# Blocks 0 and 1 of a streaming-encoder layer attended and merged as one pair, with group 1's norm and first projections woven elsewhere

## The chip, the core and the metric

The kernel runs on one core of one Trainium2 chip. The metric is the time on the device in microseconds (us), the median of several runs of the same program. TensorE is called PE below, VectorE DVE, ScalarE ACT, GpSimd POOL and SyncE SP. PE has two clock levels, 1.2 and 2.4 GHz; the profile shows the granted clock as a share of the higher one.

## What is computed

One encoder layer on 1024 frames of width 1024 (batch 1), in float32:

```python
xn = rmsnorm(x, norm1_w);  proj = xn @ w_in            # 1024 x 6656
qd, kd, vd, qc, kc, vc, gd, gc = split(proj)
o_d = diff_attention(qd, kd, vd)   # 8 heads, two softmax maps, chunk-causal, distance bias
o_c = chunk_attention(qc, kc, vc)  # 8 heads, own chunk of 64 frames and the 8 before
h = x + (sigmoid(gd + b) * (o_d @ w_branch_diff) + sigmoid(gc + b) * (o_c @ w_branch_chunk)) @ w_out
# product-key experts: 8 heads, top 16 of 128 x 128 keys, 16384 experts u, v of width 1024
q = rmsnorm(h) @ peer_wq;  s1, s2 = q_halves @ keys
e, g = top16(top16(s1) + top16(s2)), softmax of their scores
h = h + sum_k gelu(u[e_k] . rmsnorm(h)) * g_k * v[e_k]
y = rmsnorm(h, final_norm_w)
```

## The kernel before

The 1024 frames are 8 blocks of 128. `GROUPS` (line 33) makes blocks 0 and 1 group 0 and blocks 2 to 7 group 1.

*Projections.* `norm1` loads a group's rows of x through the three buffers `wr` that weights use too, norms, transposes and splits them in a high and a low part (`xh`, `xl`). `Dense` then has 52 steps per group, one for each 128 columns of `w_in`: load 512 KB of weights, split them in `wh` (ACT, line 128) and `wl` (DVE, line 129), 24 matmuls per piece of up to 512 frames (`mm3`, line 136), write the result to DRAM. `upto(n)` does the steps up to the n-th, `run()` one at each turn.

*Attention.* `attention` (line 304) works through 8 heads of the first kind and 4 head pairs of the second, for a list of blocks: scores on PE (line 347), softmax on DVE and ACT, transposes (line 203), values (line 372). `need(h)` has the projections of head h done first.

*Merge.* `merge` (line 478) takes the outputs `on` and `ocx` of its blocks through `w_bd`, `w_bc`, `w_out` (8 weight loads each; matmuls in plain float32, line 490, as many columns as it has frames; the trace holds two records for each of these matmuls), adds x, norms, and runs the 8 heads of `wq` with `top16` on DVE. `sel` runs `choose` for each block: the final top 16 and, for the blocks of `SBLK` (0, 1, 6, 7), the expert numbers `ei` (line 639).

*Experts.* Blocks 2 to 5 go through all experts densely (`gates`, `dense_experts`). Blocks 0, 1, 6, 7 gather theirs: `experts` issues 128 gathers from u and 128 from v per block on POOL (line 801), 512 KB each into five buffers, and DVE makes one product of each (lines 807 and 818). It is written at the end of the program, but a scheduler places each engine's instructions by when their inputs are ready, so the gathers of blocks 0 and 1 run from the moment that `ei` is there: 448 of them before block 6's turn, since half of block 1's v comes after block 6's u.

*The order of the work.* `weave(main, n, side, m)` runs `m` steps of a side generator over `n` steps of the main one. The order before is in the lines at the end of `layer_kernel`:

```python
weave(att_one(wk, 0, yza), 13, (dn[0].run(), 46))   # line 883
weave(merge(mp, 0, [0], yza, *ons[0]), 25, (att_one(wk, 1, yz1), 13))
run(sel([0], yza))
weave(merge(mp, 0, [1], yz1, *ons[1]), 25, (norm1(1, x1), 6))
run(sel([1], yz1))
dn[1].upto(6)
weave(att_pair(wk, 1, yza), 25, (dn[1].run(), 46))
```

Behind that come the attention of blocks 4 to 7 woven with the merge and selections of blocks 2 and 3, then the merges of blocks 4, 5 and of blocks 6, 7 (`mop`) woven with the gates, then the dense experts. Engines work through their queues in order, so an instruction that waits holds up all behind it on its engine.

Of the kernel before, what the change touches and what calls it, by code (L numbers as in the profile page):

```python
# [12 lines left out]
AF = mybir.ActivationFunctionType  # L13
OP = mybir.AluOpType

P = 128
# [35 lines left out]
def weave(main, n, *sides):  # L52

    at = [0] * len(sides)
    i = 0
    for _ in main:
        i += 1
        for k, (g, m) in enumerate(sides):
            while at[k] < m * min(i, n) // n:
                next(g, None)  # L60
                at[k] += 1
    for g, _ in sides:
        for _ in g:
            pass
# [8 lines left out]
def layer_kernel(ctx, tc, x, w1, w_in, b_gate, lq1, lk1, lq2, lk2, subln, rel,  # L73
                 w_bd, w_bc, w_out, w2, wq, keyst, u, v, ut, wf, identd, dmd, iotad, out):
    nc = tc.nc
# [4 lines left out]
    yza = ctx.enter_context(tc.tile_pool(name="yza", bufs=1))  # L80
# [11 lines left out]
    sub = con.tile([P, 1], F32, name="sub")  # L92
# [119 lines left out]
    def norm1(gi, xp):  # L212

        T = len(GROUPS[gi]) * P
        xh = xp.tile([P, KC, T], F32R, name="xh", tag="xh")
        xl = xp.tile([P, KC, T], F32R, name="xl", tag="xl")
        for i, b in enumerate(GROUPS[gi]):
            xt = wp.tile([P, KC, P], F32, name="xt", tag="wr", bufs=WBUFS).rearrange("p a b -> p (a b)")
            nc.sync.dma_start(xt, x[b * P:(b + 1) * P, :])
            xs = wp.tile([P, KC, P], F32, name="xs", tag="wl").rearrange("p a b -> p (a b)")  # L220
            ss = sm.tile([P, 1], F32, name="ss", tag="ss")
            nc.scalar.activation(xs, xt, AF.Square, accum_out=ss)
            r = rsqrt(sm, ss, 1, 1.0 / D)
            nc.scalar.activation(xs, xt, AF.Copy, scale=r)
            for g in range(2):
                o = transposes([xs[:, (4 * g + j) * P:(4 * g + j + 1) * P] for j in range(4)])
                for j in range(4):
                    c = 4 * g + j
                    oj = o[:, j * P:(j + 1) * P]
                    hi, lo = xh[:, c, i * P:(i + 1) * P], xl[:, c, i * P:(i + 1) * P]  # L230
                    nc.scalar.activation(hi, oj, AF.Copy, scale=w1c[:, c:c + 1])
                    nc.vector.scalar_tensor_tensor(lo, oj, w1c[:, c:c + 1], hi.bitcast(F32), op0=OP.mult, op1=OP.subtract)  # L232
            yield
        dn[gi].x = (xh, xl)

    class Dense:
# [24 lines left out]
        def upto(self, n):  # L261
            while self.done < min(n, len(self.steps)):
                self.steps[self.done]()
                self.done += 1

        def run(self):
            while self.done < len(self.steps):
                self.upto(self.done + 1)
                yield
# [554 lines left out]
    dn = [None, None]  # L824
    ons = {}

    def outputs(yz, T):
        return (yz.tile([P, KC, T], F32, name="on", tag="y"), yz.tile([P, 4, T], F32, name="ocx", tag="z"))

    def att_one(wk, b, yz):  # L830
        on, ocx = ons[b] = outputs(yz, P)
        yield from attention(wk, 2 * P, 0, [b], 1, lambda h: dn[0].upto(3 * h + 3),
                             lambda h, i, t: nc.scalar.activation(on[:, h, :], t, AF.Copy, scale=sub),
                             lambda h, i, t: nc.scalar.copy(ocx[:, h, :], t))

    def att_pair(wk, k, yz):
        on, ocx = ons[k] = outputs(yz, 2 * P)
        yield from attention(wk, (2 * k + 2) * P, 1, [2 * k, 2 * k + 1], 2, lambda h: dn[1].upto(3 * h + 3),
                             lambda h, i, t: nc.scalar.activation(on[:, h, :], t, AF.Copy, scale=sub),
                             lambda h, i, t: nc.scalar.copy(ocx[:, h, :], t))  # L840

# [18 lines left out]
    def sel(blocks, yz):  # L860
        for b in sorted(blocks, key=lambda b: b not in DBLK):
            yield from choose(yz, b)
# [5 lines left out]
    def pool(name):  # L868
        return tc.tile_pool(name=name, bufs=1)

    def wpool(name):
        return tc.tile_pool(name=name, bufs=2)

    with pool("x1") as x1, pool("stp") as stp:
        dn[1] = Dense(1, stp)
        dn[0] = Dense(0, stp)
        with pool("yz1") as yz1, wpool("at0") as wk:
            with pool("x0") as x0:
                run(norm1(0, x0))
                dn[0].upto(3)  # L880
                setup()
                dn[0].upto(6)
                weave(att_one(wk, 0, yza), 13, (dn[0].run(), 46))
            with pool("mp0") as mp:
                weave(merge(mp, 0, [0], yza, *ons[0]), 25, (att_one(wk, 1, yz1), 13))
                run(sel([0], yza))
                weave(merge(mp, 0, [1], yz1, *ons[1]), 25, (norm1(1, x1), 6))
            run(sel([1], yz1))
        with wpool("at1") as wk:
            dn[1].upto(6)  # L890
            weave(att_pair(wk, 1, yza), 25, (dn[1].run(), 46))
    with pool("yzb") as yzb, pool("mp") as mp:
        d1 = [k for k in range(ND) if DBLK[k] < 4]
        d2 = [k for k in range(ND) if DBLK[k] >= 4]
# [66 lines left out]
```

## Time and profile before

| | |
|---|---|
| median of 3 runs | 3340.01 us (3337.91 to 3341.29) |
| the profiled execution | 3344.66 us, span 3342.9 us |
| PE busy (matmuls; weight loads) | 3083.5 us, 92%; 2551.2 us, 76% |
| DVE busy | 2689.5 us, 80% |
| ACT busy | 1430.6 us, 43% |
| POOL busy | 1289.7 us, 39% |
| moved by DMA | 987.11 MB, 295 GB/s in the mean |
| chain that ended last | PE 71%, DVE 11%, DMA 5%, ACT 5%, issue 5% |

The span runs from the first to the last instruction on the core; the profiled execution's own time is 1.8 us longer. Busy shares are means over stages with different limits, so they say little about one stage; a table by stretches of the span does. A busy PE is not PE at its peak, because matmuls are pipelined. A wait is put down to the instruction whose signal came last.

### The profile page before, as it was taken

How to read it: one execution, taken by the hardware profiler on the slowest of the kernel's cores; microseconds unless marked ns; L12 is line 12 of the kernel's file. 1: busy time of each engine (PE TensorE's matmuls, PEld its weight loads, DVE VectorE, ACT ScalarE, POOL GpSimd, SP SyncE). 2: the span in 40 equal slices, each digit the busy share in tenths (PEclk: the TensorE clock that was granted, in tenths of full speed). 3: DMA queues.
4: the chain of work that ended last, by engine and by line, in shares of the span. 5: the costliest groups of instructions: out<-in, count | busy, mean ns of one | idle time of the engine just before them, and what ended most of it. 6: DMA issues, size and time to landing. Idle time of an engine off the chain costs nothing.

```text
span 3342.9 us, 48089 instructions
## 1 busy us (share of the span) xinstructions
PE 3083.5 (92%) x16032; PEld 2551.2 (76%) x16032; DVE 2689.5 (80%) x5720; ACT 1430.6 (43%) x2901; POOL 1289.7 (39%) x1028
## 2 busy tenths in 40 slices
PE   7987689999979988898887789999999999999998
PEld 7986578888866665577776678888888888888886
DVE  4436797787769999975785999888899888889998
ACT  6634433333323444558849833233323233223233
POOL 0000445555544442320000035555465555555553
PEclk9998899999989986899898899999999999999999
DMA  7775989999998995765444579999999999999997
GB/s 239 222 240 185 364 315 351 340 336 343 321 353 317 335 319 179 255 207 199 177 163 159 197 272 361 347 341 340 332 343 352 341 349 339 340 352 346 344 348 251
DMA packets 406120, 987.11 MB, mean 295 GB/s; under 512 B 43184, under 2 KB 188400, under 8 KB 403696
## 3 DMA queue, kind: packets, MB, share of 16 engines
q0 software_dynamic: 147456, 536.94, 45.2%
q1 hardware_dynamic: 258416, 447.11, 38.5%
q8 instruction: 126, 2.06, 0.2%
q14 instruction: 122, 1.00, 0.1%
HBM read 905.72 MB, written 78.15 MB: 294 GB/s over the span
## 4 chain that ended last, share of the span: by engine, by line
PE 71%; DVE 11%; DMA 5%; ACT 5%; issue 5%; POOL 2%; SPq 0%; DVEq 0%; POOLq 0%; ACTq 0%
PE ph L136 18%; PE mm L136 17%; PE acc L710 13%; PE mm L490 8%; PE acc L717 4%; PE sc L347 4%; PE pv L372 3%; PE tr L203 2%; POOL ge L801 2%; PE gg L669 2%; DVE junk L807 1%; ACT gst L671 1%; DMA ge<-in_u_dram,ei 1%; DVE p L353 1%; DVE iu L560 1%
## 5 line engine op out<-in xcount | busy, mean ns | idle before, releaser
L801 POOL DMA_INDIRECT ge<-in_u_dram,ei x512 | 634.0, 1238 | 1419.0 <-DVE ei L639 830.4
L801 POOL DMA_INDIRECT ge<-in_v_dram,ei x512 | 655.5, 1280 | 603.6 <-DVE acc L818 397.3
L818 DVE SCALAR_TENSOR_TENSOR acc<-ge,a,acc 128x1024 f32<-128x1024 f32 x512 | 655.6, 1280 | 24.3 <-DMA ge<-in_v_dram,ei 17.5
L807 DVE SCALAR_TENSOR_TENSOR junk<-ge,xs 128x1024 bf16<-128x1024 f32 x512 | 624.4, 1219 | 47.3 <-DMA ge<-in_u_dram,ei 41.3
L129 DVE TENSOR_TENSOR wl<-wr,wh 128x1024 fp32r<-128x1024 f32 x232 | 283.3, 1221 | 178.7 <-ACT wh L128 111.5
L128 ACT CAST wh<-wr 128x1024 fp32r<-128x1024 f32 x232 | 243.9, 1051 | 412.4 <-PE ph L136 304.4
L136 PE MATMUL ph<-x2h,wh 128*128 128x512 f32 x1024 | 400.4, 391 | 10.0 <-DVE x2l L129 7.0
L136 PE MATMUL ph<-x2l,wh 128*128 128x512 f32 x1024 | 399.8, 390 | 0.0
L136 PE MATMUL mm<-xh,wh 128*128 128x256 f32 (+1 forms) x1248 | 374.0, 325 | 0.7 <-ACT st L286 0.5
L136 PE MATMUL mm<-xl,wh 128*128 128x256 f32 (+1 forms) x1248 | 368.6, 321 | 1.2 <-DVE xl L232 1.2
L136 PEld LDWEIGHTS mm<-xh,wh 128*128 128x128 f32 x1248 | 236.3, 190 | 25.1 <-ACT st L286 3.1
L136 PE MATMUL ph<-x2h,wl 128*128 128x512 f32 x1024 | 253.9, 389 | 0.0
L136 PEld LDWEIGHTS mm<-xl,wh 128*128 128x128 f32 x1248 | 235.9, 189 | 21.2 <-DVE xl L232 1.9
L128 ACT CAST vh<-vr 128x1024 fp32r<-128x1024 f32 x128 | 128.5, 1052 | 249.5 <-PE acc L717 226.5
L136 PE MATMUL mm<-xh,wl 128*128 128x256 f32 (+1 forms) x1248 | 235.1, 324 | 0.0
L136 PEld LDWEIGHTS ph<-x2h,wh 128*128 128x128 f32 x1024 | 193.3, 189 | 51.0 <-DVE x2l L129 7.4
L136 PEld LDWEIGHTS ph<-x2l,wh 128*128 128x128 f32 x1024 | 193.3, 189 | 40.1
L136 PEld LDWEIGHTS ph<-x2h,wl 128*128 128x128 f32 x1024 | 192.2, 188 | 39.7
L347 PE MATMUL sc<-kt,qt 64*128 64x256 f32 (+3 forms) x608 | 200.5, 533 | 16.2 <-DMA kt<-kd 6.9
L128 ACT CAST ah<-ge 128x512 fp32r<-128x512 f32 x128 | 79.6, 622 | 310.0 <-DVE ge L747 309.9
L136 PEld LDWEIGHTS mm<-xh,wl 128*128 128x128 f32 x1248 | 185.2, 189 | 16.8
L710 PE MATMUL acc<-vh,ah 128*128 128x512 f32 x768 | 197.6, 389 | 0.0
(203 smaller groups left out, 5725.9 us busy)
## 6 DMA issues: line engine op xcount, KB each, us to landing
vr<-in_v_dram SPq DMA_DIRECT2D x128, 512.0 KB, 6.8
wr<-in_ut_dram SPq DMA_DIRECT2D x128, 512.0 KB, 6.1
wr<-in_w_in_dram SPq DMA_DIRECT2D x104, 512.0 KB, 5.0
gdr<-gst SPq DMA_DIRECT2D x16, 2048.0 KB, 7.8
gj<-gdr SPq DMA_DIRECT2D x512, 64.0 KB, 6.3
wr<-in_w_bd_dram SPq DMA_DIRECT2D x40, 512.0 KB, 3.8
wr<-in_w_out_dram SPq DMA_DIRECT2D x40, 512.0 KB, 7.0
wr<-in_wq_dram SPq DMA_DIRECT2D x40, 512.0 KB, 5.3
```

Of the source, the lines that this page charges most:

```text
L128: nc.scalar.copy(hi, raw)
L129: nc.vector.tensor_sub(lo, raw, hi.bitcast(F32))
L136: nc.tensor.matmul(o, w[a][:, k, :], xx[b][:, k, :], start=(i == 0), stop=(i == last))
L203: nc.tensor.transpose(o[:, i * P:(i + 1) * P], s, ident)
L347: nc.tensor.matmul(o[:, :k1 - k0], q, k[:, k0:k1], start=True, stop=True)
L372: nc.tensor.matmul(o[:, :P], aT[:, j - c, :], vt[:, v0 + j, :], start=(j == 0), stop=(j == n - 1))
L490: nc.tensor.matmul(o, w[:, k, :], xx[:, k, :], start=(k == 0), stop=(k == K - 1))
L710: nc.tensor.matmul(acc[i][hf], a[x][:, i * P:(i + 1) * P], b[y][:, hf * 512:hf * 512 + 512], **kw)
L717: nc.tensor.matmul(o, aa[:, 3 * P:4 * P], bb[:, cs], start=(n == 0), stop=(n == len(todo) - 1))
L801: nc.gpsimd.indirect_dma_start(out=t, out_offset=None, in_=src, in_offset=bass.IndirectOffsetOnAxis(ap=ei[:, k:k + 1], axis=0))
L807: nc.vector.scalar_tensor_tensor(junk, t, 1.0, xs, op0=OP.mult, op1=OP.mult, accum_out=hid[:, k:k + 1])
L818: nc.vector.scalar_tensor_tensor(acc, t, a[:, k:k + 1], acc, op0=OP.mult, op1=OP.add)
```

## The change

Blocks 0 and 1 are attended as a pair (`att_pair` with k = 0, group 0) in the first stage and merged as a pair with 256 columns. Group 1's norm is woven with that one merge. The selections of both blocks run behind it, woven with eight of group 1's projection steps (the new `some`), and the other 44 steps are woven with the attention of blocks 2 and 3. The second set of output buffers (`yz1`) goes.

```diff
--- before.py
+++ after.py
@@ -262,6 +262,11 @@
             while self.done < min(n, len(self.steps)):
                 self.steps[self.done]()
                 self.done += 1
+
+        def some(self, n):
+            for _ in range(n):
+                self.upto(self.done + 1)
+                yield
 
         def run(self):
             while self.done < len(self.steps):
@@ -827,15 +832,10 @@
     def outputs(yz, T):
         return (yz.tile([P, KC, T], F32, name="on", tag="y"), yz.tile([P, 4, T], F32, name="ocx", tag="z"))
 
-    def att_one(wk, b, yz):
-        on, ocx = ons[b] = outputs(yz, P)
-        yield from attention(wk, 2 * P, 0, [b], 1, lambda h: dn[0].upto(3 * h + 3),
-                             lambda h, i, t: nc.scalar.activation(on[:, h, :], t, AF.Copy, scale=sub),
-                             lambda h, i, t: nc.scalar.copy(ocx[:, h, :], t))
-
     def att_pair(wk, k, yz):
         on, ocx = ons[k] = outputs(yz, 2 * P)
-        yield from attention(wk, (2 * k + 2) * P, 1, [2 * k, 2 * k + 1], 2, lambda h: dn[1].upto(3 * h + 3),
+        gi = min(k, 1)
+        yield from attention(wk, (2 * k + 2) * P, gi, [2 * k, 2 * k + 1], 2, lambda h: dn[gi].upto(3 * h + 3),
                              lambda h, i, t: nc.scalar.activation(on[:, h, :], t, AF.Copy, scale=sub),
                              lambda h, i, t: nc.scalar.copy(ocx[:, h, :], t))
 
@@ -874,21 +874,17 @@
     with pool("x1") as x1, pool("stp") as stp:
         dn[1] = Dense(1, stp)
         dn[0] = Dense(0, stp)
-        with pool("yz1") as yz1, wpool("at0") as wk:
-            with pool("x0") as x0:
-                run(norm1(0, x0))
-                dn[0].upto(3)
-                setup()
-                dn[0].upto(6)
-                weave(att_one(wk, 0, yza), 13, (dn[0].run(), 46))
-            with pool("mp0") as mp:
-                weave(merge(mp, 0, [0], yza, *ons[0]), 25, (att_one(wk, 1, yz1), 13))
-                run(sel([0], yza))
-                weave(merge(mp, 0, [1], yz1, *ons[1]), 25, (norm1(1, x1), 6))
-            run(sel([1], yz1))
+        with wpool("at0") as wk, pool("x0") as x0:
+            run(norm1(0, x0))
+            dn[0].upto(3)
+            setup()
+            dn[0].upto(6)
+            weave(att_pair(wk, 0, yza), 25, (dn[0].run(), 46))
+        with pool("mp0") as mp:
+            weave(merge(mp, 0, [0, 1], yza, *ons[0]), 26, (norm1(1, x1), 6))
+        weave(sel([0, 1], yza), 18, (dn[1].some(8), 8))
         with wpool("at1") as wk:
-            dn[1].upto(6)
-            weave(att_pair(wk, 1, yza), 25, (dn[1].run(), 46))
+            weave(att_pair(wk, 1, yza), 25, (dn[1].run(), 44))
     with pool("yzb") as yzb, pool("mp") as mp:
         d1 = [k for k in range(ND) if DBLK[k] < 4]
         d2 = [k for k in range(ND) if DBLK[k] >= 4]
```

In the program as built, PE has 224 fewer merge matmuls: 448 of 128 columns become 224 of 256. SP issues 89 DMAs fewer, among them 8 loads each of `w_bd`, `w_bc`, `w_out` and `wq`. POOL's queue is the same. DVE has 4597 instructions instead of 4632. Three places show what moves.

On PE, where the first stage ends and the merge of block 0 begins (`on` and `ocx` are the two attention outputs, `wr` a weight tile, `p` and `pv` block 1's attention), before:

```order
L490 MATMUL mm<-on,wr 128x128 x8
L490 MATMUL mm<-ocx,wr 128x128 x4
L203 MATMUL tr<-ident,oh 128x128
L347 MATMUL sc<-kt,qt 128x256 x2
L203 MATMUL tr<-ident,p_2878 128x128 x2
L347 MATMUL sc<-kt,qt 128x256
L490 MATMUL mm<-on,wr 128x128 x8
L490 MATMUL mm<-ocx,wr 128x128 x4
L372 MATMUL pv<-vt,aT 128x128 x2
L347 MATMUL sc<-kt,qt 128x256 x3
```

and now, where the merge of both blocks begins:

```order
L377 MATMUL pv<-vt,aT 128x128 x2
L203 MATMUL tr<-ident,och 128x128
L495 MATMUL mm<-on,wr 128x256 x8
L495 MATMUL mm<-ocx,wr 128x256 x4
L495 MATMUL mm<-on,wr 128x256 x8
L495 MATMUL mm<-ocx,wr 128x256 x4
L495 MATMUL mm<-on,wr 128x256 x8
L495 MATMUL mm<-ocx,wr 128x256 x4
```

The attention of block 1 no longer stands between the merge's matmuls, and these have 256 columns.

On DVE, where `ei` of block 0 is made, before (`xl` is group 1's norm, `g` and `mT` the merge of block 1):

```order
L619 TENSOR_TENSOR sel<-ohib 128x64
L508 SCALAR_TENSOR_TENSOR g_4168<-g_4168,mm 128x128
L232 SCALAR_TENSOR_TENSOR xl<-tr,w1c,xh 128x128
L637 SCALAR_TENSOR_TENSOR row<-sel 128x128
L232 SCALAR_TENSOR_TENSOR xl<-tr,w1c,xh 128x128
L639 CAST ei<-row 128x128
L510 SCALAR_TENSOR_TENSOR g_4168<-g_4168,mm 128x128
L232 SCALAR_TENSOR_TENSOR xl<-tr,w1c,xh 128x128
L511 TENSOR_TENSOR mT<-g_4168 128x128
```

and now (`wl` is a weight split of group 1's projections, `p` its attention, `junk` a product of a gathered tile):

```order
L644 CAST ei<-row 128x128
L129 TENSOR_TENSOR wl<-wr,wh 128x1024
L604 SCALAR_TENSOR_TENSOR row<-s_4674,s_4673 128x128
L358 ISA p_5128,mn<-sc,dm 128x384
L358 ISA mn 128x1
L605 TENSOR_SCALAR s_4674<-row 128x128
L617 TENSOR_TENSOR ohib<-pos,iotaj 128x1024
L606 SCALAR_TENSOR_TENSOR s_4673<-row,s_4674 128x128
L395 RECIPROCAL rz_5142<-z 128x1
L619 TENSOR_TENSOR ohib<-ohib 128x1024
L608 TENSOR_TENSOR pos<-pf,s_4673 128x128
L812 SCALAR_TENSOR_TENSOR junk,hid<-ge,xs_26496 128x1024
```

It now stands behind the seventh of group 1's 52 weight splits, and before stood ahead of the first; `ei` of block 1 stands behind the eleventh, and before behind the ninth.

On DVE, in the merge of blocks 4 and 5 (`xr`) with the gates (`o`), before:

```order
L663 TENSOR_SCALAR o_13911<-iota,it_12459 128x128 x2
L521 TENSOR_TENSOR xr<-xr,tr 128x2x128
L653 TENSOR_TENSOR o_13926<-iota,it_12459 128x512
L663 TENSOR_SCALAR o_13928<-iota,it_12459 128x128 x2
L653 TENSOR_TENSOR o_13961<-iota,it_12459 128x512
L663 TENSOR_SCALAR o_13963<-iota,it_12459 128x128 x2
L521 TENSOR_TENSOR xr<-xr,tr 128x2x128
```

and the same place now (`acc` is a product of a gathered tile):

```order
L526 TENSOR_TENSOR xr<-xr,tr 128x2x128
L823 SCALAR_TENSOR_TENSOR acc<-ge,a,acc 128x1024
L658 TENSOR_TENSOR o_13328<-iota,it_11861 128x512
L668 TENSOR_SCALAR o_13330<-iota,it_11861 128x128 x2
L658 TENSOR_TENSOR o_13363<-iota,it_11861 128x512
L668 TENSOR_SCALAR o_13365<-iota,it_11861 128x128 x2
L823 SCALAR_TENSOR_TENSOR acc<-ge,a,acc 128x1024 x2
L526 TENSOR_TENSOR xr<-xr,tr 128x2x128
L658 TENSOR_TENSOR o_13380<-iota,it_11861 128x512
L668 TENSOR_SCALAR o_13382<-iota,it_11861 128x128 x2
L823 SCALAR_TENSOR_TENSOR acc<-ge,a,acc 128x1024 x2
```

Products of block 1's gathers now stand among the gates. Counted along DVE's queue, the 448 products ahead of block 6's lie so: before, 270 up to the merge of blocks 2 and 3, 140 from there to the merge of blocks 4 and 5, 38 behind that and all of them ahead of its first gate; now 210, 142 and 93, of which 42 lie ahead of the last attention block and 51 among the gates, and 3 later.

## Rows read from the trace of the kernel before

**Rows 1.** The page, part 1: busy us (share of span) x instructions.

```profile
PE 3083.5 (92%) x16032; PEld 2551.2 (76%) x16032; DVE 2689.5 (80%) x5720; ACT 1430.6 (43%) x2901; POOL 1289.7 (39%) x1028
```

**Rows 2.** Busy time by stretch: PE, PEld, DVE, ACT, POOL, granted clock, DMA share, GB/s.

```profile
24.00:198.00 174.00, 170.88 (x1389) 164.36 (x1389) 79.70 (x163) 104.13 (x242) 0.00 (x0) 1.00 0.71 222
198.00:438.00 240.00, 173.91 (x1183) 153.94 (x1183) 151.00 (x616) 96.46 (x288) 44.82 (x42) 0.87 0.78 274
438.00:966.00 528.00, 526.43 (x3053) 443.36 (x3052) 411.14 (x706) 201.19 (x417) 284.21 (x228) 1.00 0.95 335
966.00:1380.00 414.00, 350.96 (x1596) 242.56 (x1595) 370.72 (x1142) 172.68 (x414) 160.51 (x146) 0.85 0.83 285
1380.00:1474.00 94.00, 89.94 (x528) 63.83 (x527) 85.64 (x206) 53.70 (x140) 33.11 (x33) 1.00 0.82 272
1474.00:1610.00 136.00, 116.28 (x664) 102.96 (x663) 63.20 (x158) 104.92 (x247) 0.00 (x0) 0.91 0.52 179
1610.00:1930.00 320.00, 254.02 (x1467) 220.34 (x1466) 260.12 (x1139) 239.85 (x544) 0.00 (x0) 0.89 0.51 180
1930.00:3343.00 1413.00, 1395.83 (x6144) 1155.30 (x6144) 1257.00 (x1563) 441.55 (x576) 766.87 (x576) 0.99 0.94 335
```

**Rows 3.** Waits of PE, 198 to 438: us in total, times, longest.

```profile
PE tr L203 <- ACT xs L224: 19.4, 4, 7.1
PE tr L203 <- DVE xs L530: 9.8, 2, 5.7
PE sc L547 <- ACT st L542: 7.9, 4, 4.5
PE mm L490 <- DMA wr<-in_w_bd_dram: 6.8, 3, 2.9
PE mm L490 <- DMA wr<-in_w_out_dram: 5.8, 5, 1.5
```

**Rows 4.** Waits of POOL, 0 to 1000.

```profile
POOL ge L801 <- DVE ei L639: 339.8, 1, 339.8
```

**Rows 5.** PE groups, 198 to 438: count, busy us, mean ns, idle before.

```profile
L347 PE MATMUL sc<-kt,qt 64*128 64x256 f32 x40 | 11.2, 419 | 0.8 <-DMA qt<-qd 0.8
L372 PE MATMUL pv<-vt,aT 128*128 128x128 f32 x61 | 10.3, 289 | 2.1 <-ACT aT L370 1.3 <-ACT och L451 0.8
L203 PE MATMUL tr<-ident,p 128*128 128x128 f32 x14 | 3.0, 298 | 0.0
L203 PE MATMUL tr<-ident,pc 128*128 128x128 f32 x16 | 2.9, 276 | 0.1
L203 PE MATMUL tr<-ident,oh 128*128 128x128 f32 x8 | 2.5, 312 | 0.9 <-ACT oh L401 0.9
```

**Rows 6.** Busy time of line 490's matmuls alone, in two stretches.

```profile
198.00:438.00 240.00, 128.20 (x896) 118.95 (x896) 0.87 0.78 274
1380.00:1658.00 278.00, 105.27 (x446) 82.52 (x447) 0.96 0.63 217
```

**Rows 7.** Busy time of DVE, ACT, POOL on gathered tiles alone, by stretch.

```profile
438.00:966.00 528.00, 288.10 (x330) 0.00 (x0) 284.21 (x228) 1.00 0.95 335
966.00:1380.00 414.00, 177.97 (x264) 0.00 (x0) 160.51 (x146) 0.85 0.83 285
1380.00:1474.00 94.00, 48.52 (x38) 0.00 (x0) 33.11 (x33) 1.00 0.82 272
```

**Rows 8.** DVE groups, 1380 to 1610: the gather product.

```profile
L818 DVE SCALAR_TENSOR_TENSOR acc<-ge,a,acc 128x1024 f32<-128x1024 f32 x38 | 48.5, 1277 | 0.0
```

**Rows 9.** The page, part 3: the gathers' DMA queue.

```profile
q0 software_dynamic: 147456, 536.94, 45.2%
```

**Rows 10.** Busy time from 350 to 400.

```profile
350.00:400.00 50.00, 31.64 (x204) 29.19 (x205) 34.90 (x80) 25.33 (x70) 22.30 (x20) 0.83 1.01 392
```

**Rows 11.** DVE groups: a merge product of 128 columns (299 to 438), of 256 (1380 to 1610).

```profile
L508 DVE SCALAR_TENSOR_TENSOR g<-g,mm 128x128 f32<-128x128 f32 x8 | 2.3, 285 | 7.0 <-PE mm L490 6.6 <-DMA g<-gd 0.4
L508 DVE SCALAR_TENSOR_TENSOR g<-g,mm 128x256 f32<-128x256 f32 x8 | 3.3, 418 | 9.4 <-PE mm L490 9.4
```

## The prediction

> **What bounds the kernel now.** I read the page first: TensorE (PE) is busy for 92% of the span [rows 1]. That is a mean over stages, so the next view is the table of stretches [rows 2]. The reader is to see three kinds of stage there. From 24 to 198 us (group 0's projections with block 0's attention) and from 438 to 966 us (group 1's projections) PE is busy for all but 3 and 2 us: PE sets the pace, while VectorE (DVE) is busy for 80 of 174 us in the first. From 198 to 438 us, where blocks 0 and 1 are merged one after the other, PE is busy for only 174 of 240 us at a granted clock of 0.87, between its two levels of 1.2 and 2.4 GHz: it idles for 66 us. From 966 to 1380 us DVE is busy for 371 of 414 us and PE for 351. From 1474 to 1610 us there is room: DVE is busy for 63 of 136 us, the DMA engines for 0.52 of the time.
>
> What PE waits for between 198 and 438 us is in the waits [rows 3]: the normed rows of norm1 (19.4 us) and of the merge's second norm (9.8), a staged query (7.9), and weights of the 128-column matmuls (6.8 and 5.8). The expert gathers start when `ei` of block 0 is ready: POOL idled 339.8 us for it [rows 4]. From there DVE's queue holds one product per gathered tile, in a fixed order.
>
> **The change part by part.** Durations are of the profiled execution, 3344.66 us long with a span of 3342.9; the median of the runs shown is 3340.01, 4.65 lower. The sum is made against 3344.66 and the forecast is then put 4.65 lower.
>
> 1. *Attention of block 1 moves from the merge of block 0 into the first stage.* On PE it is the score, value and transpose groups, 11.2 + 10.3 + 3.0 + 2.9 + 2.5 = 30 us [rows 5]. The first stage is PE's, so all of it lies on the path there: **+30**. DVE and ACT (80 and 104 of 174 us) cover their own part of it; its loads ride on DMA engines that are busy for 0.71 of that stage [rows 2].
>
> 2. *Two merges become one.* The 896 records of line 490 with 128 columns cost 128.2 us; a pair's 446 with 256 columns cost 105.3 elsewhere, 448 would be 105.7 [rows 6]. **-22** of PE. The weights of the second merge (8 each of four matrices) are not loaded again, so each load has twice the matmul time to hide behind.
>
> 3. *PE's time from 198 to the first projection of group 1.* Busy now 174; less 30 (moved) and 22 is 122 us. Idle now 66. The weights' 13 us should shrink to about 3, the second norm's 9.8 to 5 (it happens once), the queries' 7.9 to 4, norm1's 19.4 to 15 (the same six blocks, with wider matmuls between them), and the rest, 16 in many small waits, to half. That makes 35, with bounds of 20 (norm1 hidden) and 66 (as now). So group 1's projections start at 198 + 30 + 122 + 35 = 385 instead of 438: **-53** (bounds -68 and -22).
>
> 4. *Selections woven with projections.* By the new order DVE has both selections to do before the twelfth weight split of group 1; now it has one before the tenth. In exchange no gather product stands before the eighth split. PE needs 528/52 = 10.2 us per step, so there are some 110 us for it. I charge **+4** (0 to 10) for splits that come late. 210 gather products will stand in DVE's queue ahead of the merge of blocks 2 and 3, where 270 do now. The gathers start after about seven steps, near 385 + 65 = 450, and 438 to 966 shows 228 issues in 528 us, 2.32 us each [rows 7]. From 450 to 920 that is 203, so 7 gathers could come up to 16 us late at worst; the 13 that stand behind the last split leave slack, and the charge above takes this in.
>
> 5. *From 966 to 1380.* 142 gather products stand in this stretch of DVE's queue, where there were 140: two more of 1.28 us [rows 8], on the busier engine: **+3**.
>
> 6. *The gathers pushed back.* Of the 448 gathers before block 6's, 352 have their product ahead of the mop of blocks 4 and 5, where 410 have now. The others come due in it: 42 up to the last attention block (38 now [rows 7]), 51 behind that, where POOL has no work now [rows 2]. The four cost DVE 5 us in a stretch where it is busy for 86 of 94 us: **+3**. For the 51 the trace shows no row in which gathers and gates run together, so I bound it. Below: DVE has 73 idle us and 51 x 1.28 = 65 us of products, so nothing at all. Above: 65, if no product finds a gap. In between lies the DMA engines' time. The gathers' queue took 45.2% of the span for 1024 of them [rows 9]: 0.452 x 3342.9 / 1024 = 1.476 us of all 16 engines each, 75 us for 51. The stretch itself uses 0.52 x 136 = 71. Together 146 us at a share of 1.0, 154 at the 0.95 that 438 to 966 sustains, against 136 now: +10 to +18. I take **+15**, since 0.95 is the share in the row nearest in kind (gathers beside weights).
>
> The Trainium skill, DMA: Bandwidth & Descriptors, § Bandwidth, puts the HBM limit of one core at about 358 GB/s; 179 GB/s x 136 us plus 51 x 0.524 MB is 51 MB, so by that page, an estimate, 143 us or +7. The trace shows 392 GB/s from 350 to 400 us [rows 10], above the page, so the share is used.
>
> Sum: -53 + 4 + 3 + 3 + 15 = **-28**, 3316.7 against the profiled execution and **3312** against the median. Everything from 1610 on keeps its order: the selections of blocks 6 and 7 still set when the last 576 gathers start, and the dense stage is PE's (1396 of 1413 us), so the shift reaches the end whole.
>
> **The rivals.**
> - *The gathers find room.* If the 51 products fall into DVE's and the DMA engines' gaps, and norm1's wait in the merge shrinks as well, 50 to 65 us stay: about **3283**. For it: 73 us of idle DVE from 1474 to 1610, and POOL without work from there to 1930 [rows 2]. Against it: PE (116) and ACT (105) are already near full for part of those 136 us.
> - *DVE is the bound all along, and PE's gain only makes it wait.* What DVE loses is small: 64 instructions on 128 columns at 0.285 us become 32 on 256 at 0.418 [rows 11], 4.9 us in all: **3335**. For it: DVE at 371 of 414 us from 966 to 1380, and every gather product keeps its place in that queue. Against it: from 24 to 438 DVE is idle for 183 of 414 us, and that is where the change works. The Trainium skill, Trace Analysis, § Identifying the Most-Contended Engine, would judge this way: it takes occupancy for the vector engine, sets matmul busy time aside for TensorE in favour of weight-load busy time, and has the fuller engine worked on first. By the totals [rows 1] that is DVE (80%) over weight loads (76%); the stages before 438 do not agree with it.
> - *Slower: the 51 products hold up the gates.* DVE works in order. If each one-hot of the gates and each norm waits behind a product whose gather has not landed, nothing overlaps, and the 65 us come on top: -53 + 4 + 3 + 3 + 65 = +22, **3362**. It decides from a pace on: the 43 us left before step 6's last term are used up when 51 gathers take 179 us, 3.5 us each. The slowest pace in the trace is 414/146 = 2.84 us [rows 7], which speaks against it; the small-packet gate writes beside them, which no row shows with gathers, for it.
> - *The change doing less than it says* is left out: the order shows a fifth fewer merge matmuls and merge weight loads.
>
> **How the numbers follow.** Forecast 0.50 (its own range 3296 to 3329), room for the gathers 0.22, DVE as the bound 0.16, slower 0.12. 0.2%, 6.7 us, is about what a measurement of this kernel can tell from no change: faster is below 3333.3, slower above 3346.7. Faster: 0.50 and 0.22, and a third of the 0.16, 0.77; same: the rest of it and a little, 0.12; slower 0.11. The range of 3275 to 3340 leaves out the slower case and the far end of the two beside it, about 2 in 10.
>
> **What would show it.** Right: the first 128-column merge matmuls are gone and the merge starts near 230; group 1's first projection at 375 to 400; `ei` of block 0 near 450; the stretch behind the projections about 45 to 50 us earlier; gathers running beside the gates, with 136 us there grown to about 150 and a DMA share near 0.9. Wrong: a start of group 1 after 415 (step 3's idle time was mis-sized), PE gaps behind weight splits in the first ten steps (step 4), or the gate stretch at 136 or over 180 (step 6). A dense stage of another length than 1413 us would be none of mine.

## The result, and the profile after

The changed kernel takes 3302.82 us (median of 4 runs, 3298.23 to 3305.44), the kernel before 3340.36 beside it (4 runs, 3337.91 to 3341.29). The ratio is **0.9881, with a 95% interval of 0.9868 to 0.9893**: 37.5 us faster. The forecast was 3312, with 3275 to 3340 as its range. The profiled execution took 3305.44 us, 39.2 less than that of before. Line numbers of the changed kernel are five higher behind the new `some`, from the attention to the experts (347 is now 352, 490 is 495, 496 is 501).

First the totals, from the page, part 1, of the changed kernel:

```profile
PE 3056.8 (93%) x15583; PEld 2513.9 (76%) x15583; DVE 2683.6 (81%) x5685; ACT 1418.1 (43%) x2851; POOL 1303.2 (39%) x1028
```

Beside [rows 1], DVE does the same work within 6 us, and PE 27 us less. So more time went than any engine's work did; the rest was idle time of PE. Where, the stretches show. Their cuts are the same events as in [rows 2]: end of the first stage (222), first projection of group 1 (358), last projection (896), start of the second-last merge (1307), its second group of `on` matmuls (1411), start of the last merge (1562), dense stage (1886). A merge's start is, for the last three merges, DVE's multiplication of `on`, the merge's first instruction (line 501). Columns as there.

```profile
24.00:222.00 198.00, 190.60 (x1531) 179.22 (x1531) 97.06 (x237) 127.87 (x329) 0.00 (x0) 0.99 0.68 209
222.00:358.00 136.00, 119.31 (x580) 101.07 (x581) 51.67 (x231) 53.13 (x137) 0.00 (x0) 0.92 0.54 175
358.00:896.00 538.00, 532.06 (x3065) 445.07 (x3064) 418.46 (x911) 203.87 (x422) 260.13 (x211) 0.99 0.88 309
896.00:1307.00 411.00, 344.92 (x1585) 237.08 (x1584) 372.38 (x1121) 172.38 (x417) 164.58 (x147) 0.86 0.84 290
1307.00:1411.00 104.00, 95.32 (x560) 68.89 (x560) 88.92 (x240) 58.22 (x150) 43.55 (x41) 0.98 0.84 280
1411.00:1562.00 151.00, 118.22 (x681) 104.48 (x679) 124.05 (x212) 110.92 (x256) 61.88 (x50) 0.93 0.92 343
1562.00:1886.00 324.00, 253.29 (x1422) 217.53 (x1422) 262.93 (x1138) 234.16 (x532) 0.00 (x0) 0.88 0.50 177
1886.00:3304.00 1418.00, 1397.86 (x6144) 1156.09 (x6144) 1257.03 (x1567) 441.34 (x576) 772.89 (x576) 0.99 0.94 334
```

Read it against [rows 2] line by line. The first stage grew from 174 to 198 us. The merge shrank from 240 to 136, with PE idle for 17 us of it instead of 66. Group 1's projections therefore begin 80 us earlier (358, not 438). From there the lead is given back: 10 us in the projections (538 for 528), 25 between the starts of the two last merges (255 for 230), some 4 each in the last two stages; 3 come back from 896 to 1307 (411 for 414). 80 less 40 leaves the 39 us of the profiled execution, within the rounding of the cuts.

The cut at 1411, which was at 1474, splits the 25 us into 10 and 15, but this split carries no meaning: the last attention block ends on PE 13 us behind the cut before the change and 4 us behind it now. Cut at the last attention matmul instead, before (two rows) and now (two rows):

```profile
1379.50:1487.10 107.60, 103.54 (x604) 76.07 (x604) 88.19 (x211) 55.54 (x146) 33.11 (x33) 1.00 0.79 260
1487.10:1610.20 123.10, 103.38 (x591) 91.39 (x590) 61.15 (x153) 103.45 (x242) 0.00 (x0) 0.90 0.52 180
1307.00:1414.50 107.50, 98.80 (x575) 71.67 (x574) 92.41 (x244) 58.48 (x150) 45.43 (x43) 0.98 0.84 284
1414.50:1562.20 147.70, 114.74 (x664) 101.70 (x664) 120.56 (x206) 110.85 (x255) 60.01 (x48) 0.93 0.92 343
```

By this cut the stretch up to it keeps its length and all of the 25 us lie behind it. Some merge matmuls pass from the one part to the other (PE has 29 records fewer ahead of the cut now), so the sum is what can be relied on.

What PE still waits for in the merge (222 to 358; us in total, times, longest):

```profile
PE tr L203 <- DVE xs L535: 11.8, 2, 7.2
PE mm L495 <- DVE on L501: 7.1, 1, 7.1
PE tr L203 <- ACT st L523: 1.8, 2, 1.2
PE mm L495 <- DMA wr<-in_w_bd_dram: 1.8, 1, 1.8
PE mm L495 <- DMA wr<-in_w_out_dram: 1.1, 1, 1.1
```

Of [rows 3], norm1's wait (19.4) and the queries' (7.9) are gone, the weights' fell from 12.6 to 2.9, and the merge's own second norm takes 11.8 for 9.8. The 7.1 us for `on` end at the cut: they are the attention's own norm on its way, ahead of the first merge matmul, and count to the first stage.

The price of the change stands in POOL's first wait:

```profile
POOL ge L806 <- DVE ei L644: 421.1, 1, 421.1
```

The gathers start at 421 us instead of 340 [rows 4]. So they start 81 us later where group 1 starts 80 us earlier, and 93 of the 448 products stand in DVE's queue between the starts of the two last merges, where 38 stood.

### The profile page after: what moved, and what is told of

Its sections match the earlier page's. It is cut to its first block, busy times and chain, and to the rows that moved or that the text cites. A ratio compares the mean times of both kernels' runs of the same rounds, so it can differ in the third digit from the quotient of the medians.

```text
span 3303.7 us, 46867 instructions
## 1 busy us (share of the span) xinstructions
PE 3056.8 (93%) x15583; PEld 2513.9 (76%) x15583; DVE 2683.6 (81%) x5685; ACT 1418.1 (43%) x2851; POOL 1303.2 (39%) x1028
## 4 chain that ended last, share of the span: by engine, by line
PE 61%; DVE 10%; issue 6%; DMA 5%; ACT 3%; POOL 3%; SPq 0%; DVEq 0%; POOLq 0%; ACTq 0%
PE ph L136 18%; PE acc L715 14%; PE mm L136 13%; PE acc L722 5%; PE mm L495 4%; PE sc L352 3%; POOL ge L806 3%; PE pv L377 2%; DMA ge<-in_v_dram,ei 2%; PE tr L203 2%; DVE junk L812 1%; DVE o L658 1%; DVE qs L566 1%; PE gg L674 1%; DVE iu L568 1%
## 5 line engine op out<-in xcount | busy, mean ns | idle before, releaser
L806 POOL DMA_INDIRECT ge<-in_u_dram,ei x512 | 642.3, 1255 | 1385.8 <-DVE ei L644 780.4
L352 PE MATMUL sc<-kt,qt 64*128 64x512 f32 (+3 forms) x608 | 201.3, 528 | 15.4 <-DVE mn L358 7.0
```

The costliest lines, as they stand in the source:

```text
L352: nc.tensor.matmul(o[:, :k1 - k0], q, k[:, k0:k1], start=True, stop=True)
L806: nc.gpsimd.indirect_dma_start(out=t, out_offset=None, in_=src, in_offset=bass.IndirectOffsetOnAxis(ap=ei[:, k:k + 1], axis=0))
```

## The experiments

Two theories were to be told apart. **Mine:** the wide merge makes the gain, by its matmuls and by the waits that it covers, and the gathers, started later, take part of it back among the gates. **The rival:** the gain comes from the new places of norm, selections and attention, and the gate stretch grew for a reason of its own. Unless a kernel is said to leave something out, it computes the whole result. "Merge to group 1" is the time from the first merge matmul to group 1's first projection (239.7 us before, 136.2 changed), "gate stretch" here the time between the starts of the two last merges (230.8 before, 255.3 changed), and "next merge" is the start of the first merge behind group 1's projections. The kernel before had medians of 3342.2 to 3342.91 beside the experiments; so kernels are compared by their ratios to it.

**1. The merges one by one again, all else as changed.**

```diff
-        with pool("mp0") as mp:
-            weave(merge(mp, 0, [0, 1], yza, *ons[0]), 26, (norm1(1, x1), 6))
+        with pool("yz1") as yz1, pool("mp0") as mp:
+            on, ocx = ons[0]
+            parts = [merge(mp, 0, [b], yz1, on[:, :, b * P:(b + 1) * P], ocx[:, :, b * P:(b + 1) * P]) for b in (0, 1)]
+            weave(chain(*parts), 50, (norm1(1, x1), 6))
```

> The attention of blocks 0 and 1 stays a pair, but they are merged one after the other with 128-column matmuls, the norm of the second group woven with both. Theory (the gain before group 1's projections comes from the wide merge: 22 us of matmuls and the waits for weights and for the second norm): the time from the first merge matmul to group 1's first projection, 136 us in the changed kernel, grows by 35 to 60 us, to 171 to 196, with TensorE idle 30 to 55 of it; block 0's selection is done earlier, so 56 products instead of 93 stand in the gate stretch, which gets 10 to 15 us shorter; in all 3320 to 3345. Rival (the width only saves its matmul time, and the idle time went because norm and selection were taken out of the merge): 136 grows by 20 to 25 us with idle below 22, in all 3308 to 3318.

Measured: 3341.22 us, ratio 1.0001 (0.9983 to 1.0019), so the whole gain is gone. Merge to group 1 took 201 us, somewhat over my bound. Its stretch, and PE's longest waits in it:

```profile
224.00:426.00 202.00, 145.82 (x1041) 134.35 (x1042) 107.92 (x473) 66.91 (x188) 17.98 (x19) 0.87 0.73 250
```

```profile
PE mm L495 <- DMA wr<-in_w_bd_dram: 9.6, 8, 2.0
PE tr L203 <- DVE sel L624: 8.1, 1, 8.1
PE sc L552 <- ACT st L547: 6.6, 5, 2.2
PE mm L495 <- DVE on L501: 6.3, 1, 6.3
PE tr L203 <- DVE xs L535: 5.7, 1, 5.7
```

and further down, its waits for the norm of group 1:

```profile
PE tr L203 <- DVE xl L232: 1.9, 1, 1.9
PE tr L203 <- ACT xs L224: 0.6, 1, 0.6
```

PE is busy for 27 us more than in the changed kernel and idle for 56 instead of 17: the waits for weights and staged queries of [rows 3] are back. The wait for norm1 (19.4 there) is not: the norm is woven over both narrow merges here, where it had block 1's alone, so this wait goes without the width. Group 1 starts at 426, 12 us earlier than before the change, but that is given back behind (gate stretch 237.5, and 411 us for 404 from the next merge to the second-last). Attention as a pair, norm and selections in their new places bring nothing to the total by themselves. The rival falls for this part.

**2. The norm of group 1 behind the merge instead of woven with it.**

```diff
-            weave(merge(mp, 0, [0, 1], yza, *ons[0]), 26, (norm1(1, x1), 6))
+            run(merge(mp, 0, [0, 1], yza, *ons[0]))
+            run(norm1(1, x1))
```

> The changed kernel with the norm of the second group written behind the wide merge instead of woven with it. Theory (the norm's wait, 19.4 us before the change, went because the wide matmuls cover it): the time from the first merge matmul to group 1's first projection grows from 136 to 150 to 180 us; 70 products instead of 93 stand in the gate stretch, which gives 5 to 10 us back; in all 3308 to 3340. Rival (the width of the merge alone does it, and the weaving of the norm is free either way): 130 to 145 us there, in all 3293 to 3303.

Measured: 3334.21 us, ratio 0.9975 (0.9965 to 0.9985). Merge to group 1 took 165.3 us:

```profile
225.00:390.00 165.00, 120.42 (x575) 101.98 (x576) 82.09 (x455) 50.28 (x126) 0.00 (x0) 0.83 0.47 150
```

```profile
PE tr L203 <- DVE xl L232: 32.6, 3, 12.1
PE tr L203 <- DVE xs L535: 11.0, 2, 6.0
```

PE does the same work (120 us, 119 in the changed kernel) and waits 32.6 us more for the norm's splits. The wide merge needs the norm woven into it, or most of its gain is lost; width and cover work together. As expected, fewer products then stand in the gate stretch (70 by the program, 93 in the changed kernel); it takes 239.9 us, 15 less, where 5 to 10 were expected.

**3 to 5. The 51 gathers among the gates, taken apart.** Of block 1's expert sum they leave out or replace what their expectations name.

```diff
         for k in range(K):
+            if b == 1 and 13 <= k < K // 2:
+                continue
             t = gather(v, k)
```

> The changed kernel without 51 of block 1's value gathers and their products (indices 13 to 63), so that about as many products stand between the two last merges' starts as before the change (45, where the change has 93). Theory (the pushed-back gathers lengthen the gate stretch): the time between the two starts of the last two merges, 255.3 us in the changed kernel and 230.8 before it, comes back to 230 to 236, and the total falls by about 20, to 3283. Rival (the stretch is longer for another reason, such as a merge that starts out of step with its weights): it stays at 250 to 256 and the total within 5 us of 3303. Second rival (the stretch shrinks, but a later stage takes it up, because the selections of blocks 6 and 7 or the last 576 gathers set the end): 230 to 236 there, and the total still over 3295.

```diff
-            t = gather(v, k)
+            t = xs if b == 1 and 13 <= k < K // 2 else gather(v, k)
```

> The same 51 products as in the changed kernel, each from a resident tile instead of a gathered one: VectorE's work in the gate stretch stays, the DMA engines' goes. Theory of the prediction (the DMA engines' time sets the price; VectorE has 73 idle us there for 65 us of products): the two last merges' starts are 232 to 240 us apart, the total 3283 to 3290. Rival (VectorE's time or its fixed order sets it): 248 to 256 us apart, the total 3297 to 3306.

```diff
             t = gather(v, k)
+            if b == 1 and 13 <= k < K // 2:
+                continue
             nc.vector.scalar_tensor_tensor(acc, t, a[:, k:k + 1], acc, ...)
```

> The same 51 gathers as in the changed kernel, without their products: the DMA engines' work in the gate stretch stays, VectorE's goes. Theory of the prediction (the DMA engines' time sets the price): the two last merges' starts are 246 to 256 us apart, the total 3295 to 3305. Rival (VectorE): 230 to 238 us apart, the total 3281 to 3288. If both of the two halves give nearly all of the gain back, each alone fits and it is the two together that do not.

Measured: 3279.49 us without both (ratio 0.9815, 0.9795 to 0.9836), 3286.89 with the products (0.9837, 0.9814 to 0.986), 3288.84 with the gathers (0.984, 0.9822 to 0.9858). The gate stretch in the four traces, in the order changed kernel, neither, products alone, gathers alone (columns as in the stretches above):

```profile
1307.00:1562.00 255.00, 213.54 (x1239) 173.37 (x1238) 212.97 (x450) 169.14 (x405) 105.44 (x91) 0.95 0.89 317
```

```profile
1311.00:1543.00 232.00, 208.45 (x1224) 169.46 (x1223) 156.43 (x404) 163.22 (x396) 44.96 (x41) 0.96 0.68 233
```

```profile
1313.00:1552.00 239.00, 210.49 (x1213) 172.74 (x1212) 214.48 (x452) 163.50 (x392) 44.04 (x41) 0.94 0.67 228
```

```profile
1309.00:1555.00 246.00, 212.34 (x1213) 170.70 (x1212) 156.89 (x403) 163.09 (x393) 96.00 (x92) 0.94 0.90 332
```

Without the 51 the stretch is back at 232 (230.8 before), and the 23 us reach the end (22 by the ratios). So they are the cause of the longer gate stretch. The gathers alone cost 13 or 14 us of it, at a DMA share of 0.90, about what the DMA sum of step 6 had given for both. The products alone, with DVE busy for 214 of 239 us and the DMA engines at 0.67, cost 6 or 7. Both theories were half right: the products alone came out within the bounds of mine, the gathers alone (245.6 us, 3288.84) below mine and above the rival's. The gathers price more, but DVE's 58 us of products are not free though it had room on paper. On PE the price shows in the wait for the last-but-one merge's second norm, which stands in DVE's queue, in the changed kernel and without the 51:

```profile
PE tr L203 <- DVE xs L535: 14.7, 2, 7.9
PE tr L203 <- DVE xs L535: 6.5, 2, 5.4
```

Alone the two cost 13.3 and 6.4 us, 19.7 in sum, and together 23.0. That they cost more together is not shown: experiments 6 and 7 have the same 51 gathers and products in the stretch, and it takes 251.3 and 252.3 us there, 19 to 20 more than without them.

**6. The selections first, six projection steps ahead of the attention.**

```diff
-        weave(sel([0, 1], yza), 18, (dn[1].some(8), 8))
+        run(sel([0, 1], yza))
         with wpool("at1") as wk:
-            weave(att_pair(wk, 1, yza), 25, (dn[1].run(), 44))
+            dn[1].upto(6)
+            weave(att_pair(wk, 1, yza), 25, (dn[1].run(), 46))
```

> The changed kernel with the two selections written ahead of group 1's projections as before the change, with six projection steps and then the attention of blocks 2 and 3; all else as changed. Theory (the weaving of the selections is worth little, because TensorE's projections need nothing of them and VectorE's order stays nearly the same): group 1's projections take 537 to 550 us to the start of the next merge (547 in the changed kernel), in all 3298 to 3308. Rival (the weaving is what keeps TensorE busy behind the merge): TensorE loses 15 to 30 us in the first 90 us of group 1, in all 3315 to 3335.

Measured: 3296.71 us, ratio 0.987 (0.9851 to 0.9889), an interval that overlaps the changed kernel's. The weaving of the selections is worth nothing that can be seen. As built, a kernel with six steps woven into the selections instead of behind them is this same program, instruction by instruction, so the weaving itself changes nothing. What is left is the number of steps ahead. The first row is the changed kernel from group 1's first projection to the next merge, the second this one:

```profile
358.00:906.00 548.00, 532.98 (x3071) 445.78 (x3069) 422.61 (x915) 204.34 (x423) 264.94 (x215) 0.99 0.88 310
```

```profile
359.00:900.00 541.00, 525.95 (x3066) 443.17 (x3064) 421.94 (x911) 201.55 (x422) 271.87 (x215) 0.99 0.89 314
```

PE is busy for 7 us less with the same work. Among the kernels with the changed merge, all six traces with eight steps (the changed kernel, experiments 3 to 5, 8 and 9) have 545.5 to 548.6 us here, the three with six steps (6, 10 and 11) 540.7 to 543.5: 2 to 8 us between them. The count alone is not the cause, though: experiment 1 has eight steps too and took 537.1, experiment 2 552.7, with gathers that start at other times. Of the 7 us 4.4 lie in the attention's score matmuls, line 352 (columns PE, PEld, granted clock, DMA share, GB/s), with eight steps and with six:

```profile
358.00:906.00 548.00, 37.21 (x128) 14.40 (x128) 0.99 0.88 310
```

```profile
359.00:900.00 541.00, 32.76 (x128) 12.88 (x128) 0.99 0.89 314
```

These are the same 128 matmuls, 487 ns long in the mean in both and 62 us in sum, so they overlap one another less with eight steps. PE's order differs: it has them in 38 unbroken runs with eight steps, in 34 with six. Over all traces the busy time follows the runs: 32.8 to 33.8 us with 34 runs, 35.4 with 36, 36.5 with 37, 36.8 to 37.2 with 38. What else the length of the stretch depends on (537.1 in experiment 1, with 37 runs) stays open.

**7. Four steps ahead.** As number 6, with `upto(4)` and 48 steps woven.

> The kernel with the selections first, but four projection steps instead of six ahead of the attention of blocks 2 and 3 (48 woven with it instead of 46); the changed kernel has eight. Theory (with six steps the time from group 1's first projection to the next merge was 540.7, with eight 547.4, because the attention's VectorE work starts late and stands behind the last projections): with four it falls by another 3 to 8 us, in all 3288 to 3295. Rival (the 7 us were the noise of one profiled execution, or the limit is elsewhere by now): 538 to 544 us, in all 3295 to 3303.

Measured: 3296.31 us, ratio 0.9856 (0.984 to 0.9872), and 543.6 us from group 1's first projection to the next merge. My theory of a steady gain falls: four steps do no better than six. Its score matmuls take 36.8 us, in 38 runs, near those with eight steps, which speaks for the order of PE's queue and not for the number of steps by itself. PE's waits in the stretch are alike.

**8. The 51 gathers behind the last merge's gated sum.** They take their numbers from a copy of `ei` that DVE writes as 0 times a slice of that sum, plus the numbers:

```diff
         # (in choose)
+            if b == 1:
+                ef1.append(...)
+                nc.vector.tensor_copy(ef1[0], ef.rearrange("p a b -> p (a b)"))
         # (in merge, behind the loop over mT)
+        if blocks[-1] == 7:
+            ...
+            nc.vector.scalar_tensor_tensor(eif, mT[:, KC - 1, 0:P], 0.0, ef1[0], op0=OP.mult, op1=OP.add)
+            ...
+            nc.vector.tensor_copy(eib, eif)
+            ef1.append(eib)
         # (in gather)
-            ... ap=ei[:, k:k + 1] ...
+            ... ap=(ef1[1] if b == 1 and src is v and 13 <= k < K // 2 else ei)[:, k:k + 1] ...
```

> The changed kernel, whole, with the 51 gathers of block 1 that stand among the gates (indices 13 to 63) made to wait for the last merge's gated sum: they take a copy of their index that is written behind it, so they run from about 1660 on, where the changed kernel has VectorE busy for 62 of 120 us (1680 to 1800) and the DMA engines for 0.40. Theory (the place of these gathers is what costs 23 us, not their number): the two last merges start 232 to 238 us apart, the stretch from there to the dense stage grows from 324 to 326 to 338 us, in all 3282 to 3293. Rival (DMA and VectorE have no cheaper place; what the gates lose the last merge pays): the stretch to the dense stage grows by 18 us or more, in all 3298 to 3310.

Measured: 3296.44 us, ratio 0.9862 (0.9846 to 0.9879), between the two theories, with an interval that overlaps the changed kernel's. The stretches from the start of the second-last merge to the dense stage:

```profile
1312.00:1544.00 232.00, 208.10 (x1227) 169.62 (x1226) 156.91 (x405) 163.74 (x397) 44.84 (x41) 0.96 0.69 235
1544.00:1679.00 135.00, 117.50 (x663) 102.02 (x662) 125.62 (x569) 82.44 (x188) 10.11 (x9) 0.95 0.59 204
1679.00:1879.00 200.00, 140.01 (x794) 120.89 (x793) 185.54 (x573) 158.35 (x357) 52.12 (x42) 0.83 0.77 278
```

The gate stretch is back at 231.2 us, and the stretch behind it loses 11 (335.2 from the last merge's start to the dense stage, 324.0 in the changed kernel). There DVE is now busy for 186 of 200 us, with the last merge's top-16 work in the same queue. By the stretches (24 us back, 11 lost) the later place is cheaper, not free; in the total, 6 us by the ratios, this is not clear of the noise.

**9. Sixteen of the 51 into the dense stage.** `if k == K // 2` becomes `if k == 48`.

> The changed kernel with 16 of the 51 gathers moved behind block 6's first 128, so into the dense stage. Theory of room (the dense stage is TensorE's, with the DMA engines at 0.94 and VectorE at 0.89 of it): the gate stretch gets about 7 us shorter and the dense stage stays at 1403, in all 3294 to 3299. Rival (the gathers' even pace in the dense stage, 2.36 us each, sets its end as much as TensorE does): 16 more take 38 us, the dense stage grows by 15 to 38 us, in all 3310 to 3335.

Measured: 3316.36 us, ratio 0.9927 (0.991 to 0.9944): by the ratios 15 us slower than the changed kernel, though its dense stage starts 14 us earlier. The dense stage, and what follows its last matmul:

```profile
1872.00:3273.00 1401.00, 1396.23 (x6144) 1154.88 (x6144) 1252.32 (x1559) 430.72 (x541) 784.72 (x584) 1.00 0.95 338
3273.00:3307.00 34.00, 0.00 (x0) 0.00 (x0) 24.63 (x22) 11.22 (x36) 9.77 (x8) 0.56 0.71 249
```

PE's dense stage keeps its length, but the last gathers, their products and the last norms run on for 34 us with PE idle, where it is 14 in the changed kernel. The rival holds: the gathers keep a pace of 2.36 us (592 from 1893.3 to 3292.0 us, as 576 from 1911.5 to 3272.2 in the changed kernel), and 576 of them just fit beside the matmuls.

**10 to 12. The two edits together.** Number 6 with 26 (10) or 38 (11) of the 51 gathers late, and number 7 with 26 (12).

> Selections first with six steps, and 26 of the 51 gathers (indices 38 to 63) behind the last merge's gated sum; the other 25 stay among the gates. Theory (both places cost more per gather the more they hold: 51 cost 23 us among the gates and about 15 behind them): half and half costs about 8 + 4 us, the last two merges start 238 to 244 us apart, 320 to 326 from there to the dense stage, in all 3280 to 3289. Rival (the price of a gather is the same in either place, 0.3 to 0.45 us, whatever else runs): 18 to 20 us together, in all 3289 to 3296.

> The same with 38 of the 51 late and 13 among the gates. Theory (each place has room for some of them): 234 to 240 us and 322 to 330 us, in all 3281 to 3290, no better than 26 late if the late place fills up from some 30 on. Rival (a constant price): 3288 to 3294.

> Four steps ahead of the attention, and 26 of the 51 gathers late: the two edits together. If they act in stages of their own, their gains add: 3276 to 3286. If four steps bring nothing over six: 3280 to 3289, as with six.

Measured: 3293.23 us (ratio 0.9854, 0.9837 to 0.987), **3285.89** (0.983, 0.9813 to 0.9846) and 3292.59 (0.9845, 0.9828 to 0.9861). Number 11 is faster than both kernels: 57 us under the one before, and its interval lies wholly below the changed kernel's. Its stretches from the start of the second-last merge to the dense stage:

```profile
1299.00:1537.00 238.00, 209.94 (x1220) 170.39 (x1219) 171.07 (x415) 163.12 (x395) 59.60 (x54) 0.95 0.74 255
1537.00:1658.00 121.00, 103.22 (x581) 89.39 (x581) 117.03 (x556) 75.13 (x170) 0.40 (x1) 0.94 0.54 185
1658.00:1757.00 99.00, 69.88 (x395) 61.58 (x394) 81.95 (x141) 80.89 (x187) 46.37 (x38) 0.85 0.87 325
1757.00:1869.00 112.00, 82.08 (x481) 70.64 (x482) 105.88 (x482) 84.92 (x187) 1.50 (x1) 0.80 0.59 208
```

The 38 late gathers are done by 1757, before the stretch in which DVE is busy for 106 of 112 us; with all 51 late they ran on to 1807. That this is why 38 beat 51 is only argued. Less than half of its lead over number 6 lies where the late gathers act: of the 12.5 us between the two profiled executions 5 are between the second-last merge's start and the dense stage, the rest in the attention behind group 1's projections and in the dense stage. The expectation on 26 was wrong: its stretches came about as foreseen (238.3 and 326.2 us), its total 4 us above the bound and within the rival's; in the profiled executions 26 and 38 reach the dense stage within 1.2 us of each other, so the 7 us between their medians lie in the dense stage or between runs, and stay open. With 38 late the last stretch took 331.5 us, 1.5 above its bound. Number 12 lies above both its bounds; four steps add nothing to six.

## Why the prediction was right, and where its steps were off

The forecast's mechanism held: PE's matmul and idle time in the merge were the gain, the later gathers the price, and most of the shift reached the end. Against -28 the profile gives -39.2. That the total came so near is in part luck: the gain of step 3 was put 27 us too low, and the losses of steps 4 and 6 and on the way to the end 21 too low. By its own steps:

1. *Attention of block 1, +30.* **Too much.** PE's busy time in the first stage grew by 20 us and the stage by 24; the other 4 are idle time, from the 7.1 us at its end that wait for `on`. The step added busy times of groups [rows 5], and those overlap. The first stage after shows it:

```profile
L136 PE MATMUL mm<-xh,wh 128*128 128x256 f32 x412 | 104.4, 291 | 0.0
L136 PE MATMUL mm<-xl,wh 128*128 128x256 f32 x414 | 102.0, 284 | 0.3 <-DVE xl L232 0.3
L136 PE MATMUL mm<-xh,wl 128*128 128x256 f32 x416 | 62.9, 287 | 0.0
```

These three alone make 269 us in a stretch where PE is busy for 190.6 in all. So the sum of the groups' busy times overstates what they add.

2. *Two merges into one, -22.* **Right.** Line 495's matmuls take 105.0 us from 222 to 358, where line 490's took 128.2 [rows 6]: -23. The converse in experiment 1 costs 19 us there (123.6), and 27 us of PE in all.

3. *Start of group 1, -53.* **Its idle time was mis-sized**, and this made most of the error: -80, beyond its bound of -68. Busy time was right (119 for 122), but idle time 17, below the bound of 20, where I took 35. I had left norm1 15 of its 19.4 us because its blocks stayed the same; with twice the matmul time between two of them the wait went to nothing. Experiment 1 shows that it is this time and not the width (0.6 us of that wait with narrow merges), experiment 2 what the cover is worth: 32.6 us of waiting without it. The other terms: weights 2.9 for 3, queries 0 for 4, the small waits 2 for 8, and against these the second norm 11.8 for 5.

4. *Weaving, +4.* Measured +10 from group 1's first projection to the next merge (547.4 for 537.7), and **for another reason**: no wait behind a weight split shows among PE's waits there, and the weave itself moves nothing (experiment 6). With two steps fewer ahead of the attention 2 to 8 us of it are gone, some 4 of them by the order of the score matmuls.

5. *966 to 1380, +3.* Measured -2 to -3: nothing to tell.

6. *The pushed-back gathers, +3 and +15.* The sum was **too low**: +24.5 in the gate stretch for 18. Without the 51 the stretch is 1.5 us longer than before the change (experiment 3), so hardly anything is left for the four products of the +3, and the 51 cost 23 us for 15. The DMA sum was right for the gathers by themselves (13 us of experiment 5). That DVE's products cost nothing because DVE had 73 idle us was wrong: they cost 6 us alone and 6 to 10 beside the gathers (experiments 6 and 7, and the changed kernel).

The shift from 1610 on did not reach the end whole: 4 us went on the way to the dense stage and 4 in it. Experiment 3 shows the first 4 to be the gathers' too (319.8 us there without them, 324.0 with); the dense stage's 4 were not explained: from its first matmul to the end of the span the traces of the experiments, number 9 apart, have 1412.5 to 1417.4 us.

Of the rivals, *gathers find room* (3283) is what experiment 11 nearly reaches by an edit of its own, not what this change does. *DVE is the bound all along* (3335) is out: DVE's total is 2683.6 against 2689.5, and the time fell by 37.5 us. So the rule of the Trainium skill, Perfetto Trace Analysis, § Identifying the Most-Contended Engine, to work on the fullest engine first, would by the totals have missed this gain: DVE's total hardly changed, while by stages PE lost 49 idle us in the merge. *The gates held up* (3362) did not come: the stretch with the 51 gathers took 151 us, under the 179 from which it would have decided. The Trainium skill, DMA: Bandwidth & Descriptors, § Bandwidth, with 358 GB/s, its limit of one core and what it gives each of two that stream at once, made the part from 1474 on 143 us by estimate, the DMA share 154; the trace has 151 us at 343 GB/s and a share of 0.92, which is nearer to the share.

## What to carry to other kernels

When a stage waits for weights, norms and staging in small pieces, doubling the columns of its matmuls can buy more than its matmul time: here also the waits for weights and staged queries went. Side work such as the next norm is covered when enough matmul time lies between its pieces; woven over the wide merge or over both narrow ones it cost PE next to nothing, behind the merge 32.6 us. Then look at what the stage used to release, since work that starts later (here the gathers) lands in another stage; count that stage's load on every engine it uses. The overflow can be moved to a stretch with more room by a data dependence, if the scheduler would not wait, but the room there must be measured too: of 24 us 11 came back as a loss. Do not add up the busy times of PE's groups: they overlap.

## What was not expected of the hardware

The same score matmuls, of the same length each, took PE 32.8 to 37.2 us in group 1's projections, depending on how PE's queue broke them into runs; a small edit to the weave moved the time by 4 us at the same granted clock of 0.99. And gathers were not hidden by idle time on paper: 51 of them cost 13 us with DVE busy for 157 of 246 us and the DMA engines at 0.90, and their products alone 6 us with DVE busy for 214 of 239 us.
